# Block attention of the last two mixers: high and low parts in 128-column products, one query block at a time, x kept in DRAM in between

## The chip, the cores and the metric

The kernel runs on one core of one Trainium2 chip. The metric is device time in microseconds (us) of one launch. All data are float32 at the interface. A product that needs float32 accuracy is mostly made here from high and low parts: each operand is split into hi (rounded to the engine's fp32r format) and lo (the rest), and hi x hi, hi x lo and lo x hi are summed in PSUM.

## The reference, cut to what matters

The model has two blocks of two layers each. The change touches the two layers of the second block, whose mixer is a hybrid of three parts. The third part, `nsa_mixer`, is attention with 8 query heads in 2 key groups (4 heads per group, 64 wide), 512 positions, in 4 query blocks of 128. Each query block has three branches: compressed keys (31 of them), selected blocks and a window. With 512 positions, 8 selected blocks of 64 and a window of 512, both latter branches come down to causal attention over all earlier keys.

```python
def hybrid_mixer(h, w_in, ...):
    p = h @ w_in
    za, qb, kb, vb, gb, qc, kcm, vcm, ksl, vsl, kwn, vwn, gc = jnp.split(p, splits, axis=-1)
    y_a = spatial_gating_mixer(za, ...)
    y_b = retention_mixer(qb, kb, vb, gb, ...)
    y_c = nsa_mixer(qc, kcm, vcm, ksl, vsl, kwn, vwn, gc, ...)
    return jnp.concatenate([y_a, y_b, y_c], axis=-1) @ w_out

# in nsa_mixer, for each query block of 128:
p_cmp = masked_softmax(q . k_cmp, ...)   ; o_cmp = p_cmp . v_cmp
p_sel = masked_softmax(q . k_sel, m_sel) ; o_sel = p_sel . v_sel
p_win = masked_softmax(q . k_win, m_win) ; o_win = p_win . v_win
o = g0 * o_cmp + g1 * o_sel + g2 * o_win
```

## The kernel before, in words

The kernel is written for a scheduler that fixes the order of each engine's instructions when it is built; at run time each engine works through its own list in order and waits on semaphores. Activations are kept transposed: 128 features on the partitions by 512 positions, in tiles of 128x512 out of one pool of 71 (names `a`). PSUM has 8 banks of 128x512 (names `p`). Weights come through a ring of raw tiles (`wr`) that ScalarE (ACT) casts to `wh` and VectorE (DVE) completes with `wl`; SyncE (SP) issues nearly all loads, in order.

`hybrid()` does one mixer. It loads five tables (L1413, 256 KB each) and the compression weights `c_w1` (L1423, four of 256 KB), which GpSimd (POOL) multiplies by position columns (L1679) and DVE reduces (L1683). Then come the projections by w_in, and `nsa()`, in which attention runs in steps. A step is a query block `i` and a branch `b` (selected or window): `scores` of one key group, the other work of the mixer (gating, retention: the generator `rest`), the `values` of the step before, scores of the other group, and the softmax (`exponentials`, `weights`). A string `cnt` of digits says how many pieces of `rest` are put at each place, called by `fill()`.

`values(i, b, ...)` walks over the key tiles of 128 keys. For each tile and each key group g it transposes four heads of probabilities (L1790) into one bank, copies the bank to SBUF (L1792, g 0 on ACT, g 1 on DVE) and multiplies by 64 columns of values in plain float32, with the result of both groups in one bank `out[i]`. There are 20 such key tiles in a layer (1+2+3+4 for each of two branches). `blocks(i)` does the compressed branch's scores with 32 keys in high and low parts, `finish(i, ...)` adds its values to `out[i]` and writes `y` as hi (ACT) and lo (DVE). The steps run in the order (3,0), (0,0), (3,1), (1,0), (0,1), (2,0), (2,1), (1,1), so up to three banks `out[i]` are open at a time. `late()` is work that may run beside the last values: the first column tiles of the product by w_out. `post_ln` then takes x, which has been in 8 tiles of SBUF all along (its first use there is a multiplication of `x[0]` on DVE), adds the mixer's result and normalises it.

Of the kernel before, what the change touches and what calls it, by code (L numbers as in the profile page):

```python
# [15 lines left out]
P = 128  # L16
# [87 lines left out]
class Net:  # L104
    def __init__(self, ctx, tc, t):
        self.tc, self.nc, self.t = tc, tc.nc, t
        self.pool = ctx.enter_context(tc.tile_pool(name="sb", bufs=1))
        self.psum = ctx.enter_context(tc.tile_pool(name="ps", bufs=8, space=bass.MemoryType.PSUM))
        self.n = 0
        self.cols = {}  # L110
        self.bg = []
# [1296 lines left out]
    def hybrid(self, l, rhs, first, nxt, start):  # L1408
# [18 lines left out]
        kc = [kcs[:, i * 32:i * 32 + 32] for i in range(4)]  # L1427
# [12 lines left out]
        pb = self.position_parts(l, w1)  # L1440
        q = []
# [34 lines left out]
        both, vals, gt = [self.A(), self.A()], [], self.pool.tile([P, 96], F32, name=self.name("g"), tag="gates", bufs=1)  # L1476

        def others_of_nsa():
            keys(2560)
            yield  # L1480
            for j, ps in enumerate(self.gemm_tok(w, [(2432, 128), (2688, 152)], rhs)):
                o = both[j // 2][:, j % 2 * 256:j % 2 * 256 + 256]
                nc.scalar.copy(o, ps[:, :256])
                vals.append((o[:, :P], o[:, P:]))
                self.act(gt[:, j * 24:j * 24 + 24], ps[:, 256:280], AF.Tanh, scale=0.5)
            self.ts(gt, gt, 0.5, MUL, 0.5, ADD)
            yield
# [15 lines left out]
        def late():  # L1503
            for _ in rest:
                pass
            yield from self.begin(t["w_out2"][l], [(0, 2 * P)], mix, begun, rows=rows)
# [197 lines left out]
    def compressed_heads(self, hid, w2, kc):  # L1704
# [11 lines left out]
        self.doubled(ps[:, :32], *kc)  # L1716
# [21 lines left out]
    def nsa(self, q, kk, vals, gt, kc, vz, tab, ready, rest, late):  # L1738
# [45 lines left out]
        def values(i, b, probs, out):  # L1784
            for kt in range(i + 1):
                pts = []
                for g in range(2):
                    ps = self.PS()
                    for r in range(4):
                        nc.tensor.transpose(ps[:, q4[r]], probs[g][r][:, q4[kt]], self.const("ident"))  # L1790
                    pts.append(self.A())
                    (nc.vector.tensor_copy if g else nc.scalar.copy)(pts[g], ps)  # L1792
                for g in range(2):
                    self.mm(out[group[g], :], vals[kt][b][:, group[g]], pts[g], b == 0 and kt == 0, False, True)
                yield

        def blocks(i):
# [4 lines left out]
            pr, nm, sm = self.A()[:, :256], self.S(8), self.S(8)  # L1802
            for g in range(2):
                ps = self.PS()
                for r in range(4):
                    self.products(ps[:, r * 32:r * 32 + 32], q[r][g], kc, g, q4[i], slice(0, 32), True, True)
                self.tt(r3(pr[:, g * P:g * P + P]), r3(ps[:, :P]), mk(cadd, 4), ADD)
# [10 lines left out]
        def finish(i, pr, out):  # L1818
# [5 lines left out]
            for r in range(4):  # L1824
                for g in range(2):
                    self.mm(out[group[g], q4[r]], vz[:, g * 256 + r * 64:g * 256 + r * 64 + 64],
                            pt[:, g * P:g * P + P], False, r == 3, True)
            if not y:
# [3 lines left out]
                y.extend((self.A(F32R), self.A(F32R)) for _ in range(2))  # L1832
            for r in range(4):
                hi, lo = y[r][0][:, q4[i]], y[r][1][:, q4[i]]
                nc.scalar.copy(hi, out[:, q4[r]])
                self.tt(lo, out[:, q4[r]], hi.bitcast(F32), SUB)


        steps = [(3, 0), (0, 0), (3, 1), (1, 0), (0, 1), (2, 0), (2, 1), (1, 1)]
        before, out, cmp_ = None, {}, {}  # L1840
        cnt = iter("0200112003110110200111000110020301001101")
# [5 lines left out]
        for step in steps + [None]:  # L1847
# [4 lines left out]
            if before:  # L1852
                i, b, probs = before
                if b == 0:
                    out[i] = self.PS()
# [122 lines left out]
```

## Time and profile before

| | |
|---|---|
| median of 3 runs | 3577.85 us (3575.04 to 3580.2) |
| profiled execution | 3580.52 us |
| its span, first to last instruction | 3578.8 us |
| TensorE (PE) busy | 98% |
| VectorE (DVE) busy | 59% |
| ScalarE (ACT) busy | 38% |
| mean granted TensorE clock | 0.992 |

The two hybrid mixers' attention lies at 2261.5 to 2460 us and 2952.5 to 3150 us of the span, some 198 us each. PE is busy through the whole kernel, so a time is saved where PE has less to do, or waits less.

### The profile page before, as it was taken

Reading aid. Unit: us, or ns where it says so; the run is one execution under the profiler, and the core shown is the slowest. Engines: PE = TensorE matmul, PEld = TensorE weight load, DVE = VectorE, ACT = ScalarE, POOL = GpSimd, SP = SyncE. Lnnn points to the kernel's source line nnn. Section 1 sums busy time; section 2 is a strip of 40 time slices with the busy share of each in tenths; the row PEclk is TensorE's granted clock in tenths of the full one; section 3 lists DMA queues with packets and bytes.
Section 4 is the critical chain, followed back from the end, with each engine's and each line's share of the span. In section 5 each row is a group of like instructions: output and inputs, shape, how many; then the busy total and the mean of one; then the engine's idle time right before and its main releaser. Section 6 shows DMA issues by size and latency. Waiting matters only on the chain. (4 is left out here: it accounts for less than half of the span.)

```text
span 3578.8 us, 50232 instructions
## 1 busy us (share of the span) xinstructions
PE 3505.2 (98%) x20564; PEld 2880.8 (80%) x20564; DVE 2127.5 (59%) x3451; ACT 1347.1 (38%) x2198; POOL 143.2 (4%) x189
## 2 busy tenths in 40 slices
PE   8999999999999999999999999999999999999999
PEld 7888877788888888888788888767888887678887
DVE  4442677655434866377676636656655456566565
ACT  3232443223322322257632223543543255445431
POOL 0000000000000000000000001000100020010000
PEclk9999999999999999999999999999999999999999
DMA  4332310013323565321156634211332341013322
GB/s 137 95 96 81 111 43 24 15 60 106 99 95 95 183 188 185 91 77 52 55 149 185 190 112 123 66 31 42 92 97 93 96 113 54 24 54 106 96 98 78
DMA packets 348855, 338.88 MB, mean 95 GB/s; under 512 B 20182, under 2 KB 326929, under 8 KB 348625
## 3 DMA queue, kind: packets, MB, share of 16 engines
q1 hardware_dynamic: 347280, 332.46, 30.7%
q0 software_dynamic: 1344, 3.21, 0.3%
q8 instruction: 161, 2.64, 0.3%
q14 instruction: 70, 0.57, 0.0%
HBM read 333.53 MB, written 2.10 MB: 94 GB/s over the span
## 5 line engine op out<-in xcount | busy, mean ns | idle before, releaser
L152 PE MATMUL p<-a,wh 128*128 128x512 f32 (+1 forms) x8524 | 2430.5, 370 | 18.1 <-ACT a L137 6.2
L152 PEld LDWEIGHTS p<-a,wh 128*128 128x128 f32 x8524 | 1544.9, 190 | 303.2 <-issue 22.6
L152 PE MATMUL p<-a,wl 128*128 128x512 f32 (+1 forms) x4262 | 1564.5, 368 | 0.0
L140 DVE TENSOR_TENSOR wl<-wr,wh 128x1024 fp32r<-128x1024 f32 (+2 forms) x556 | 639.0, 1152 | 730.4 <-ACT wh L252 706.0
L152 PEld LDWEIGHTS p<-a,wl 128*128 128x128 f32 x4262 | 810.2, 190 | 132.4 <-issue 2.7
L252 ACT CAST wh<-wr 128x1024 fp32r<-128x1024 f32 (+2 forms) x518 | 517.3, 1000 | 951.0 <-PE p L152 899.9
L140 DVE TENSOR_TENSOR a<-a,a 128x512 f32<-128x512 f32 (+8 forms) x745 | 439.6, 604 | 89.3 <-ACT a L156 59.8
L152 PE MATMUL p<-a,a 64*64 64x64 f32 (+9 forms) x4360 | 408.0, 275 | 12.6 <-ACT a L1792 3.4
L152 PEld LDWEIGHTS p<-a,a 64*64 64x64 f32 (+3 forms) x4360 | 269.2, 148 | 106.3 <-issue 49.0
L137 ACT ACTIVATE a<-a 128x512 f32<-128x512 f32 (+1 forms) x347 | 194.0, 590 | 344.4 <-DVE a L140 240.1
L140 DVE TENSOR_TENSOR a<-p,a 128x512 f32<-128x512 f32 (+5 forms) x334 | 203.8, 623 | 79.7 <-PE p L152 64.8
L152 PE MATMUL p<-wh,a 128*128 128x256 f32 (+2 forms) x992 | 231.1, 324 | 0.1
L156 ACT CAST a<-a 128x512 fp32r<-128x512 f32 x148 | 91.3, 619 | 269.2 <-DVE a L140 267.2
L152 PEld LDWEIGHTS p<-wh,a 128*128 128x128 f32 x992 | 167.6, 190 | 18.2 <-issue 4.0
L152 PE MATMUL p<-wl,a 128*128 128x256 f32 (+2 forms) x496 | 160.1, 323 | 0.0
L143 DVE SCALAR_TENSOR_TENSOR acc<-wr,s,acc 128x1024 f32<-128x1024 f32 x84 | 107.8, 1283 | 86.3 <-DMA wr<-in_w_ada 86.3
L143 DVE SCALAR_TENSOR_TENSOR a<-p,cols,a 128x510 f32<-128x510 f32 (+1 forms) x176 | 125.1, 744 | 50.8 <-ACT a L137 49.5
L140 DVE TENSOR_TENSOR a<-a,p 128x256 f32<-128x256 f32 (+1 forms) x256 | 116.1, 480 | 34.8 <-PE p L152 34.1
L137 ACT ACTIVATE a<-p 128x512 f32<-128x512 f32 (+2 forms) x152 | 79.6, 551 | 77.3 <-PE p L152 71.5
L152 PEld LDWEIGHTS p<-wl,a 128*128 128x128 f32 x496 | 94.2, 190 | 8.2 <-issue 0.7
L137 ACT ACTIVATE a<-a,cols 128x256 fp32r<-128x256 f32 (+3 forms) x140 | 73.8, 550 | 53.7 <-DVE a L140 53.7
L137 ACT ACTIVATE a<-p,cols 128x512 f32<-128x512 f32 x92 | 68.5, 771 | 59.2 <-PE p L152 59.1
(200 smaller groups left out, 1698.5 us busy)
## 6 DMA issues: line engine op xcount, KB each, us to landing
wr<-in_l_ffn_w_in SPq DMA_DIRECT2D x176, 512.0 KB
wr<-in_w_ada SPq DMA_DIRECT2D x96, 512.0 KB
wr<-in_w_up SPq DMA_DIRECT2D x88, 512.0 KB
wr<-in_l_ffn_w_out SPq DMA_DIRECT2D x68, 512.0 KB
wr<-in_w_in SPq DMA_DIRECT2D x40, 512.0 KB
wr<-in_w_down SPq DMA_DIRECT2D x39, 512.0 KB
wr<-in_l_w_qkv SPq DMA_DIRECT2D x24, 512.0 KB
wr<-in_l_w_in SPq DMA_DIRECT2D x22, 512.0 KB
```

Source lines behind the costliest of these rows:

```text
L137: self.nc.scalar.activation(out, in_, func, bias=bias, scale=scale)
L140: self.nc.vector.tensor_tensor(out, a, b, op=op)
L143: self.nc.vector.scalar_tensor_tensor(out, a, s, b, op0=op0, op1=op1)
L152: self.nc.tensor.matmul(out, lhsT, rhs, start=start, stop=stop, skip_group_check=skip)
L156: self.nc.scalar.copy(hi, src)
L252: self.nc.scalar.copy(hi[:, :m], raw[:, :m])
```

## The change

`values` splits the transposed probabilities into hi (ACT) and lo (DVE) and multiplies both by 128 columns per group: 64 columns of the values' hi beside 64 of their lo. Each group has its own bank, so `out[i]` is two banks, whose two halves are added in `finish` (an ACT copy and a DVE addition) before `y` is split. `blocks` holds the compressed keys as hi beside lo, 64 columns, so that one query tile times 64 columns takes the place of two times 32. The steps run block by block, with a new `cnt`. x is written to DRAM (`away`) at the mixer's start and read back in `late()`.

```diff
+        self.dram = ctx.enter_context(tc.tile_pool(name="dr", bufs=1, space=bass.MemoryType.DRAM))
...
-        kc = [kcs[:, i * 32:i * 32 + 32] for i in range(4)]
+        kc = [kcs[:, i * 64:i * 64 + 64] for i in range(2)]
...
         pb = self.position_parts(l, w1)
+        away = self.dram.tile([D, T], F32, name=self.name("away"))
+        for k in range(KD):
+            nc.sync.dma_start(away[k * P:(k + 1) * P, :], self.x[k])
...
-                o = both[j // 2][:, j % 2 * 256:j % 2 * 256 + 256]
-                nc.scalar.copy(o, ps[:, :256])
-                vals.append((o[:, :P], o[:, P:]))
+                o = self.A(F32R)
+                ov = o.rearrange("p (b g s d) -> p g s b d", b=2, g=2, s=2)
+                pv = ps[:, :256].rearrange("p (b g d) -> p g b d", b=2, g=2)
+                for g in range(2):
+                    nc.scalar.copy(ov[:, g, g], pv[:, g])
+                    self.tt(ov[:, g, 1 - g], pv[:, g], ov.bitcast(F32)[:, g, g], SUB)
+                vals.append((o[:, :256], o[:, 256:]))
...
+            self.x = [self.A() for _ in range(KD)]
+            for k in range(KD):
+                nc.sync.dma_start(self.x[k], away[k * P:(k + 1) * P, :])
             yield from self.begin(t["w_out2"][l], [(0, 2 * P)], mix, begun, rows=rows)
...
-                    pts.append(self.A())
-                    (nc.vector.tensor_copy if g else nc.scalar.copy)(pts[g], ps)
+                    pts.append(self.split(ps))
                 for g in range(2):
-                    self.mm(out[group[g], :], vals[kt][b][:, group[g]], pts[g], b == 0 and kt == 0, False, True)
+                    for u, part in enumerate(pts[g]):
+                        self.mm(out[g], vals[kt][b][:, g * P:g * P + P], part, b == 0 and kt == 0 and u == 0, False, True)
...
+            ps = self.PS()
             for g in range(2):
-                ps = self.PS()
                 for r in range(4):
-                    self.products(ps[:, r * 32:r * 32 + 32], q[r][g], kc, g, q4[i], slice(0, 32), True, True)
-                self.tt(r3(pr[:, g * P:g * P + P]), r3(ps[:, :P]), mk(cadd, 4), ADD)
+                    o = (g * 4 + r) * 64
+                    self.mm(ps[:, o:o + 64], q[r][g][:, q4[i]], kc[g], o == 0, False, True)
+            parts = ps.rearrange("p (r u n) -> p u r n", u=2, n=32)
+            self.tt(r3(pr), parts[:, 0], mk(cadd, 8), ADD)
+            self.tt(r3(pr), parts[:, 1], r3(pr), ADD)
...
+            o = self.A()
+            for g in range(2):
+                nc.scalar.copy(o[group[g]], out[g][group[1 - g]])
+                self.tt(o[group[g]], out[g][group[g]], o[group[g]], ADD)
             for r in range(4):
                 hi, lo = y[r][0][:, q4[i]], y[r][1][:, q4[i]]
-                nc.scalar.copy(hi, out[:, q4[r]])
-                self.tt(lo, out[:, q4[r]], hi.bitcast(F32), SUB)
-        steps = [(3, 0), (0, 0), (3, 1), (1, 0), (0, 1), (2, 0), (2, 1), (1, 1)]
+                nc.scalar.copy(hi, o[:, q4[r]])
+                self.tt(lo, o[:, q4[r]], hi.bitcast(F32), SUB)
+        steps = [(i, b) for i in (1, 2, 3, 0) for b in range(2)]
-        cnt = iter("0200112003110110200111000110020301001101")
+        cnt = iter("00011111111111110111101111011001101111000")
```

In the changed kernel the helper `split` stands at L155, its cast at L157 and its subtraction at L141; the transposes at L1803, the store of x at L1445, its reload at L1518, and the tables' and `c_w1`'s loads at L1414 and L1424.

Of the PE list of the first hybrid mixer, one place in `values` where two key tiles follow each other. Before (`p_19325`, `p_19332`, `p_19341`, `p_19348` take transposes, `p_19324` is `out[i]`):

```order
L1790 MATMUL p_19332<-consts,a_19139 128x128
L152 MATMUL p_19324<-a_19330,a_19013 64x512
L152 MATMUL p_19324<-a_19337,a_19013 64x512
L1790 MATMUL p_19341<-consts,a_19035 128x128
L1790 MATMUL p_19341<-consts,a_19038 128x128
L1790 MATMUL p_19341<-consts,a_19041 128x128
L1790 MATMUL p_19341<-consts,a_19044 128x128
L1790 MATMUL p_19348<-consts,a_19130 128x128
```

And after, at such a place (`p_20089`, `p_20098`, `p_20111`, `p_20120` take transposes; `p_19828` and `p_19829` are the two banks of `out[i]`):

```order
L153 MATMUL p_19828<-a_20094,a_19237 128x512
L153 MATMUL p_19829<-a_20103,a_19237 128x512
L153 MATMUL p_19828<-a_20095,a_19237 128x512
L1803 MATMUL p_20111<-consts,a_19877 128x128
L1803 MATMUL p_20111<-consts,a_19880 128x128
L1803 MATMUL p_20111<-consts,a_19883 128x128
L1803 MATMUL p_20111<-consts,a_19886 128x128
L153 MATMUL p_19829<-a_20104,a_19237 128x512
L1803 MATMUL p_20120<-consts,a_19980 128x128
```

Two plain float32 products became four in high and low parts, of which the last (lo of group 1, `a_20104`) stands behind the next key tile's first four transposes.

Of the SP list, the head of the first hybrid mixer. Before, the tables and `c_w1` follow three loads of w_in:

```order
L236 DMA wr_18724<-in_w_in 128x8x128
L1413 DMA a_18583<-in_hybrid_tab 128x512
L1413 DMA a_18584<-in_hybrid_tab 128x512
L1413 DMA a_18585<-in_hybrid_tab 128x512
L1413 DMA a_18586<-in_hybrid_tab 128x512
L1413 DMA a_18587<-in_hybrid_tab 128x512
L1423 DMA a_18593<-in_c_w_k 128x8x64
L1423 DMA a_18594<-in_c_w_k 128x8x64
```

After, seven of the eight stores of x stand between; the last three of them, and what follows, are:

```order
L1445 DMA away_18629<-a_131 128x512
L1445 DMA away_18629<-a_138 128x512
L1445 DMA away_18629<-a_145 128x512
L1414 DMA a_18585<-in_hybrid_tab 128x512
L1414 DMA a_18586<-in_hybrid_tab 128x512
L1414 DMA a_18587<-in_hybrid_tab 128x512
L1414 DMA a_18588<-in_hybrid_tab 128x512
L1414 DMA a_18589<-in_hybrid_tab 128x512
L1424 DMA a_18595<-in_c_w_k 128x8x64
L1424 DMA a_18596<-in_c_w_k 128x8x64
```

Each store waits until DVE has written its tile of x, so the loads behind wait for that too.

Of the DVE list, the end of the first hybrid mixer. Before, `a_101` and `a_108` are x in SBUF, and the four `y` rows are the last lo parts:

```order
L1823 COPY a_20864<-p_20861 128x256
L147 TENSOR_SCALAR a_20918<-a_101 128x512
L147 TENSOR_SCALAR a_20921<-a_108 128x512
L140 TENSOR_TENSOR wl_21026<-wr_21023,wh_21025 128x1024
L140 TENSOR_TENSOR y_19959<-p_20025,y_19959 128x128
L140 TENSOR_TENSOR y_19960<-p_20025,y_19960 128x128
```

After, `a_20957` and `a_20958` are x read back from DRAM:

```order
L1839 COPY a_20996<-p_20993 128x256
L141 TENSOR_TENSOR wl_21175<-wr_21172,wh_21174 128x1024
L141 TENSOR_TENSOR a_21006<-p_20820,a_21006 64x512
L141 TENSOR_TENSOR a_21006<-p_20821,a_21006 64x512
L148 TENSOR_SCALAR a_21067<-a_20957 128x512
L148 TENSOR_SCALAR a_21070<-a_20958 128x512
L141 TENSOR_TENSOR y_19700<-a_21006,y_19700 128x128
```

Two additions that join the halves of `out` stand there now, and the reloaded x is asked for ahead of the last lo parts.

## Rows read from the trace of the kernel before

**Rows 1.** The page: busy us, share of the span and instructions of each engine.

```profile
PE 3505.2 (98%) x20564; PEld 2880.8 (80%) x20564; DVE 2127.5 (59%) x3451; ACT 1347.1 (38%) x2198; POOL 143.2 (4%) x189
```

**Rows 2.** Windows, both attention stretches: us, busy (x) by engine, PEclk, DMA share, GB/s.

```profile
2261.50:2460.00 198.50, 193.50 (x1144) 133.04 (x1144) 124.13 (x297) 94.31 (x245) 7.85 (x6) 0.99 0.13 35
2952.50:3150.00 197.50, 191.85 (x1144) 132.69 (x1143) 123.63 (x292) 94.29 (x245) 7.85 (x6) 1.00 0.13 35
```

**Rows 3.** PE groups by form, 2261.5 to 2460: xcount | busy, mean ns | idle before.

```profile
L152 PE MATMUL p<-a,a 128*64 128x512 f32 x80 | 35.1, 638 | 1.8 <-ACT a L1792 1.7
L1790 PE MATMUL p<-consts,a 128*128 128x128 f32 x160 | 22.8, 278 | 2.2 <-ACT a L137 1.5 <-ACT a L1792 0.7
...
L152 PE MATMUL p<-a,a 128*128 128x32 f32 x64 | 8.2, 267 | 0.0
```

**Rows 4.** The same view, 2952.5 to 3150.

```profile
L152 PE MATMUL p<-a,a 128*64 128x512 f32 x80 | 33.7, 616 | 2.5 <-ACT a L1792 1.7 <-DVE a L1792 0.6
```

**Rows 5.** Timeline of PE: start, us, line, operation, count, [idle before].

```profile
2300.46 0.62 PE L152 MATMUL p<-a,wh 128*128 128x512 f32 x2
...
2301.16 0.62 PE L152 MATMUL p<-a,wh 128*128 128x512 f32 x2
...
2301.93 2.42 PE L152 MATMUL p<-a,a 128*64 128x512 f32 x8
2304.28 0.73 PE L152 MATMUL p<-a,wh 128*128 128x512 f32 x2
...
2325.33 1.86 PE L152 MATMUL p<-a,a 128*128 128x32 f32 x16
...
2401.21 1.04 PE L1790 MATMUL p<-consts,a 128*128 128x128 f32 x8
2402.49 1.62 PE L152 MATMUL p<-a,a 128*64 128x512 f32 x4 [0.24 <-ACT a L1792]
2404.04 1.09 PE L1790 MATMUL p<-consts,a 128*128 128x128 f32 x8
```

**Rows 6.** ACT and DVE groups by form, 2261.5 to 2460.

```profile
L1792 ACT COPY a<-p 128x512 f32<-128x512 f32 x20 | 11.5, 584 | 35.2 <-PE p L1790 35.2
...
L1792 DVE COPY a<-p 128x512 f32<-128x512 f32 x20 | 13.6, 687 | 8.0 <-PE p L1790 8.0
L1764 DVE TENSOR_REDUCE s<-p 128x1 f32<-128x512 f32 x16 | 10.4, 684 | 3.8 <-PE p L152 3.8
...
L140 DVE TENSOR_TENSOR a<-p,a 128x512 f32<-128x512 f32 x10 | 6.7, 688 | 1.9 <-PE p L152 1.8
```

**Rows 7.** Timelines of SP, POOL, DVE and PE at the head of the first hybrid mixer.

```profile
2183.65 2.73 SPq L1413 DMA_DIRECT2D a<-in_hybrid_tab  x5
...
2198.60 4.25 POOL L1679 TENSOR_TENSOR a<-a,cols 128x512 f32<-128x512 f32 x4
...
2197.17 5.97 DVE L140 TENSOR_TENSOR a<-a,a 128x256 fp32r<-128x256 f32 x3
...
2206.85 1.08 DVE L140 TENSOR_TENSOR a<-a,a 128x256 f32<-128x256 f32 x3
...
2223.31 4.06 DVE L1683 TENSOR_REDUCE a<-a 128x64 f32<-128x512 f32 x4
...
2202.01 0.58 PE L152 MATMUL p<-a,wh 128*128 128x256 f32 x1 [1.34 <-DVE a L140]
...
2205.11 1.14 PE L152 MATMUL p<-a,wh 128*128 128x256 f32 x2 [0.39 <-ACT a L453]
```

**Rows 8.** Windows, the head of the first hybrid mixer (columns as in Rows 2).

```profile
2196.80:2262.00 65.20, 62.49 (x411) 54.93 (x411) 41.52 (x63) 27.27 (x45) 9.07 (x14) 0.92 0.31 83
```

**Rows 9.** Timelines of POOL and DVE at the head of the second hybrid mixer.

```profile
2909.09 4.07 POOL L1679 TENSOR_TENSOR a<-a,cols 128x512 f32<-128x512 f32 x4
...
2912.20 0.68 DVE L1670 COPY st<-p 64x512 f32<-64x512 f32 x1 [5.84 <-PE p L152]
```

**Rows 10.** DMA view of 2180 to 2240: GB/s in 40 slices of 1.5 us.

```profile
GB/s 259 112 249 283 389 366 319 231 218 119 60 161 82 147 0 11 0 0 0 0 0 11 279 248 255 256 0 0 11 0 0 0 0 0 212 143 159 191 239 65
```

More of the change, by code (lines that the diff above doesn't have):

```diff
@@ L1475, in hybrid @@
         vz = self.compressed_heads(hid, w2, kc)
-        both, vals, gt = [self.A(), self.A()], [], self.pool.tile([P, 96], F32, name=self.name("g"), tag="gates", bufs=1)
+        vals, gt = [], self.pool.tile([P, 96], F32, name=self.name("g"), tag="gates", bufs=1)
         def others_of_nsa():
@@ L1715, in compressed_heads @@
                 self.mm(pv[r * 32:r * 32 + 31, g * 64:g * 64 + 64], hid[64:128, cs], w2[64:128, 0:64])
-        self.doubled(ps[:, :32], *kc)
+        self.doubled(ps[:, :32], *[kc[g][:, i * 32:i * 32 + 32] for i in range(2) for g in range(2)])
         vzv = vz.rearrange("p (g r d) -> p g r d", g=2, r=4)
@@ L1825, in finish @@
                 for g in range(2):
-                    self.mm(out[group[g], q4[r]], vz[:, g * 256 + r * 64:g * 256 + r * 64 + 64],
+                    self.mm(out[g][group[g], q4[r]], vz[:, g * 256 + r * 64:g * 256 + r * 64 + 64],
                             pt[:, g * P:g * P + P], False, r == 3, True)
@@ L1854, in nsa @@
                 if b == 0:
-                    out[i] = self.PS()
+                    out[i] = self.PS(), self.PS()
                 work = values(i, b, probs, out[i])
```

## The prediction

> **What bounds the kernel now.** I began with the page: PE is busy for 98% of the span, DVE for 59%, ACT for 38% [rows 1]. So only PE's own work, or a wait on PE, is worth anything, and the other engines count where PE stands behind them. Then I read the windows of the two attention stretches, which hold nearly all that the change touches. There PE is idle for 198.5 - 193.5 = 5.0 us and 197.5 - 191.85 = 5.65 us, at a clock of 0.99 and 1.00 [rows 2]. That idle time is not the whole of the waiting: a matmul's row also covers what it waits for inside a group, and for that I went to the groups by form [rows 3, 4] and to starts in the timeline [rows 5]. Last I read the head of the first mixer, where the clock is only 0.92 [rows 8].
>
> What the groups show: the values' products (64 columns by 512) cost 35.1 us of busy time in the first layer and 33.7 in the second, in 80 rows for 40 products, so one plain float32 product leaves two rows [rows 3, 4]. They have the only waits on the eviction copies.
>
> **Values, PE's work.** Eight such rows back to back take from 2301.93 to 2304.28, 2.35 us, 0.294 each [rows 5]. So 80 cost 23.5 us with nothing to wait for. After, a layer has 80 products of 128 columns by 512 in fp32r. Of that kind three take from 2300.46 to 2301.16, 0.70 us, 0.233 each [rows 5]; 80 cost 18.7. PE's work falls by 4.8 us a layer.
>
> **Values, the waits.** A lone key tile now goes: eight transposes at 2401.21, a wait of 0.24, four product rows at 2402.49, the next at 2404.04 [rows 5]. The products take 1.55 us where 4 x 0.294 = 1.18 is work, so 0.24 + 0.37 = 0.61 us is waiting. Over 20 key tiles that is 12.2 us a layer, and values with their waits cost 23.5 + 12.2 = 35.7.
>
> After, each bank of transposes gives two tiles, hi by ACT and then lo by DVE, which reads hi. I price hi at ACT's copy of the same shape, 0.584, and lo at DVE's subtraction out of PSUM, 0.688 [rows 6]. The copy now ends some 1.25 us after the first transpose starts (2402.49 - 2401.21 = 1.28 with the start of the product). From there, at full clock: the first product (hi, group 0) starts at 1.28; hi of group 1 is ready at 1.83, so the second starts at 1.87; lo of group 0 is ready at 1.94, so the third follows at once at 2.10; lo of group 1 is ready at 2.63. The order puts the next tile's transposes or scores ahead of that fourth product, 0.44 us or more, so it starts at 2.77 and waits for nothing. The waits are 0.40 behind the transposes and 0.36 ahead of the second product, 0.76 us for a tile with nothing between. Where scores or other products lie between transposes and products, as at many tiles in the new order, both shrink. For the second of two tiles in a row the same walk gives 0.61. I take 0.6 a tile, between 0.4 and 0.76: 12 us a layer. Values after cost 18.7 + 12 = 30.7, so 5 us less a layer, 10 in all. The bounds from 0.4 and 0.76 are 9 and 1.8 us less a layer.
>
> **Blocks.** Sixteen of the 32-column products take 1.86 us, 0.116 each [rows 5]; there are 64 a layer [rows 3], 7.4 us. Of 64 columns there will be 32. The trace has no such row, but the transposes with 128 columns take 1.04 / 8 = 0.13 at most [rows 5], so a price between 0.116 and 0.13 holds: 3.7 to 4.2 us. I take the nearer, 0.116: 3.7 us less a layer. The added DVE additions are few (one of 128x256 a block in place of two halves' worth) and stand in front of a softmax that is used a step later, so I cost them at nothing; if that cover is gone, each is under 0.69 us, 2.8 us a layer.
>
> **The added ACT and DVE work.** A layer gets 20 more evictions on each engine: 40 casts in place of 20 copies on ACT, 40 subtractions in place of 20 copies on DVE. With the splits of the values and the joins of `out`, ACT goes from 94.3 to about 111 us and DVE from 124.1 to about 144 of some 190 [rows 2, 6]. DVE's subtractions stand in its list among the score reductions (0.684 each) [rows 6] and the scalings; behind a late subtraction wait PE's fourth product and the next step's softmax. The waits of PE on DVE and ACT in the softmax (1.5 us of the transposes' 2.2 idle is on the scaling, ACT's L137) [rows 3] can grow. I put 1.5 us a layer on that, from 0 to 5.
>
> **The end of a query block.** `finish` gets two copies on ACT and two additions on DVE ahead of `y`, 2 x 0.584 and 2 x 0.688 at most, with the second copy beside the first addition about 1.9 us. The order puts twelve products by w_out (12 x 0.233 = 2.8 us) between the last values and the first use of the last `y`. So I cost it at nothing; without that cover it is 1.9 us a layer. For the other three query blocks `y` is not needed for a long time.
>
> **x through DRAM.** 2 MB go out and 2 MB come back in a layer. In the attention stretches DMA is 0.13 busy [rows 2], so there is room. The reload stands ahead of one w_out load in SP's list and can start when the last gate column's products are done; from there PE has about 35 products of 512 columns and some 100 short ones up to the last `y`, 35 x 0.233 plus some 9, about 17 us. At the 319 to 389 GB/s that four slices in a row moved at the head [rows 10], 2 MB take 5.4 to 6.6 us. Hidden, at nothing. The stores at the head push the tables and `c_w1` back: they were issued from 2183.65 [rows 7], and now wait for x, on which DVE still works in the row at 2206.85 [rows 7]. With the stores that is 4.3 MB, 11 to 14 us at that rate, much of it ahead of the last store, so the weights of the compression land near 2213 instead of before 2198.60, when POOL starts on them. What needs them is POOL's multiplication and then the reductions on DVE, which start at 2223.31 [rows 7], so PE does not see it.
>
> **The head.** One thing gains there. DVE's three additions of 128x256 at 2197.17 last 5.97 us where three of the same size take 1.08 later [rows 7]. They are stuck exactly while POOL multiplies (2198.60 to 2202.85) [rows 7], and PE waits 1.34 on DVE and 0.39 on ACT behind it [rows 7]. In the second mixer POOL's multiplication falls into a DVE gap of 5.84 us and holds up nothing [rows 9]. With `c_w1` later, POOL's work moves to about 2215, past this tail. The gain is at least those two waits, 1.73 us, and at most the 4.9 us by which DVE's op is too long; I take 3, once. The Trainium skill (SBUF — State Buffer, section "Who interferes with whom") says that a DVE instruction with two SBUF inputs and a GpSimd instruction that reads SBUF lock each other out for a whole instruction. The trace agrees with the one lock that it shows. By that rule the multiplication, once moved, would hold up whatever two-input work of DVE is then under way, the `wl` subtractions for w_in, by up to its own 4.25 us, and if PE had no slack there the head's gain would be spent and the time by the median would be 3564.
>
> **The sum.** Values -10, blocks -7.4, engines' load +3, head -3: -17.4 us. Nearly all of it, (4.8 + 3.7) x 2 = 17, is work that PE no longer has; the waits on both sides come out alike. On the profiled execution's 3580.5 that gives 3563. That execution lies 2.7 us above the median of the three runs, so by the runs' median 3577.85 it is 3560. The forecast's own range, from the bounds above, is 3550 to 3570.
>
> **Rivals.** *The evictions become the wait.* For it: every key tile now passes through two engines in series, 0.584 + 0.688 twice, in lists that also carry the softmax. Against it: lo of group 1 is ready ahead of its use in the walk above, and DVE still has a quarter of its time free. PE saves (4.8 + 3.7) x 2 + 3 = 20 us apart from waits; over 40 key tiles that is 0.5 us a tile. If the wait grows from 0.61 to about 1.1 us a tile, which one score reduction (0.684) ahead of most lo parts would do, nothing is left: 3571 to 3585. The Trainium skill (Perfetto Trace Analysis, section "Matmuls") asks to rotate PSUM banks so that evictions overlap with the next group's products. Here a transposed bank is held until its lo is done, and `out` takes two, which speaks for this rival; no row of the kernel before shows a wait for a bank.
>
> *Slower.* The same DVE list decides: from 1.3 us a tile on, two reductions ahead of each lo, the kernel is slower; at 1.5 us it is (1.5 - 1.1) x 40 = 16 us, 3594. For it: in a softmax step DVE gets four reductions at once. Against: now the g 1 copy on DVE stands in the same list and costs only 0.37 a tile.
>
> *The parking of x holds up the loads.* The w_in loads stand behind all stores and table loads. If they land more than 9 us later than now in each layer, PE waits for them, and the gain is gone; at 15 us it is 3590. The rate in [rows 10] speaks against it.
>
> *A larger gain.* If other work covers the tiles' waits wholly, values cost 18.7 of 35.7 us: -34, -7.4, -3 is 3533; halfway it is 3545. For it: the new string puts a piece of other work at nearly every place, and the first steps have only two key tiles, so that the first wait (1.5 us, on scalings) shrinks.
>
> **Chances.** Forecast 0.52; larger gain 0.22; evictions eat it 0.14; slower by DVE's list 0.07; slower by the parked x 0.05. What a measurement of this kernel can tell from no change is about 0.2%, 7 us. Faster is the first two, 0.74; the same 0.14; slower 0.12. The range leaves about a tenth on each side: half of the larger gain below 3543, and most of the slower cases above 3582.
>
> **What will show it.** In the windows of the attention stretches the span should fall by 5 to 10 us a layer; the values' group should read 128x512, 80 a layer, with 0.6 us a tile of waiting in their starts; 32 products of 64 columns near 0.116; DVE near 145 us. At the head DVE's three additions near 1.1 us, and POOL's row near 2215. If the scores or transposes wait on DVE where they did not, the first rival holds; if PE waits on `wh` or `wl` soon after the head, the third; if DVE stands before the first scaling of x in `post_ln` for a DMA, the reload is late. I am wrong above all if the walk through one tile misses what stands ahead of lo in DVE's list.

## The result, and the profile after

The changed kernel takes 3620.97 us (median of 4 runs, 3614.46 to 3628.54) against 3578.57 of the kernel before (4 runs): a ratio of 1.0121 with a 95% interval of 1.0109 to 1.0133. It is 42 us slower where 18 us less were forecast. Its profiled execution has a span of 3626.8 us.

The windows of the head of the first mixer and of its attention (us, busy us and instructions of PE, PEld, DVE, ACT and POOL, granted clock, DMA share, GB/s), kernel after:

```profile
2183.00:2262.00 79.00, 76.52 (x536) 69.36 (x535) 48.74 (x97) 34.15 (x63) 12.62 (x21) 0.98 0.51 145
2262.00:2470.00 208.00, 182.64 (x1036) 138.99 (x1035) 134.97 (x308) 103.67 (x262) 7.76 (x6) 0.88 0.14 42
2276.00:2312.00 36.00, 25.55 (x123) 18.66 (x122) 28.20 (x81) 15.79 (x47) 4.87 (x5) 0.67 0.11 30
2312.00:2450.00 138.00, 127.52 (x713) 93.88 (x712) 84.63 (x180) 68.96 (x163) 0.00 (x0) 0.95 0.12 34
2450.00:2475.00 25.00, 20.57 (x113) 16.38 (x112) 17.51 (x50) 11.73 (x37) 2.89 (x1) 0.73 0.19 70
```

Beside [rows 2], PE is now idle for 208 - 182.64 = 25.4 us in the attention, where it was 5.0 in a stretch of much the same length, and the granted clock there is 0.88 in place of 0.99. More than half of the idle time and most of the lost clock lie at the two ends: in the first 36 us PE is idle for 10.5 us at a clock of 0.67, in the last 25 for 4.4 at 0.73. The 138 us between lose another 10.5 at 0.95. DVE and ACT are far from full, as forecast.

The stage is longer by about what the whole kernel lost. The first transpose of the first mixer's attention starts at 2281.12 (before, 2285.30), the first load of w_up behind that mixer is issued at 2490.65 (before, 2468.27): 209.5 us in place of 183.0. In the second mixer it is 207.5 in place of 182.2, so the two stages lose some 52 us, where the spans of the profiled executions differ by 48.0; the first stage starts 4.2 us earlier. The groups of PE by form in the first attention, kernel after, 2262 to 2505 (columns as in [rows 3]), show where it waits:

```profile
L153 PE MATMUL p<-a,a 128*128 128x512 f32 x120 | 49.1, 485 | 11.1 <-ACT a L157 9.0 <-DVE a L141 1.4 <-ACT a L138 0.6
...
L1803 PE MATMUL p<-consts,a 128*128 128x128 f32 x160 | 27.4, 312 | 4.3 <-ACT a L138 3.6 <-DVE a L141 0.6
...
L153 PE MATMUL p<-a,a 128*128 128x384 f32 x32 | 9.6, 414 | 3.1 <-ACT a L1783 2.9
```

The first row holds the 80 new products (and 40 others of the same shape): 9.0 us of waiting on the casts to hi (L157), where the old products waited 1.7 on ACT's copies [rows 3]. The second is mostly the transposes' wait for the softmax's scaling on ACT, which grew from 1.5 [rows 3] to 3.6. The third are scores that wait until ACT's exponentials (L1783) have emptied a bank; no score waited for that before.

How such a wait comes about is seen in the timelines of PE, ACT and DVE at the first step's values, kernel after (the third row is PE at the last step's):

```profile
2281.12 1.94 PE L1803 MATMUL p<-consts,a 128*128 128x128 f32 x8 [2.69 <-ACT a L138]
...
2285.53 1.65 PE L153 MATMUL p<-a,a 128*128 128x512 f32 x4 [1.85 <-ACT a L157]
...
2468.20 0.80 PE L153 MATMUL p<-a,a 128*128 128x512 f32 x1 [3.14 <-ACT a L157]
...
2282.24 0.59 ACT L157 CAST a<-p 128x512 fp32r<-128x512 f32 x1
2284.59 0.42 ACT L138 ACTIVATE a<-a 128x256 f32<-128x256 f32 x1 [1.75 <-DVE a L141]
2284.91 0.57 ACT L157 CAST a<-p 128x512 fp32r<-128x512 f32 x1
...
2283.33 0.43 DVE L141 TENSOR_TENSOR a<-a,s 128x256 f32<-128x256 f32 x1 [0.84 <-POOL s L1548]
```

The second cast to hi does not follow the first. Between them stands an activation of the gating (the "other work" that the string of fills put there), which waits 1.75 us on DVE, which in turn waits on POOL. The cast's data are ready (the eight transposes of the row at 2281.12 end at 2283.06); its place in ACT's list is not. PE waits 1.85 us for it. At the last step it is the same: the cast stands behind two casts of other work, for which ACT waits 3.07 us on DVE, and PE waits 3.14.

### The profile page after: what moved, and what is told of

Read it like the earlier page. It is cut to its first block, busy times and chain, and to the rows that moved or that the text cites. A ratio compares the mean times of both kernels' runs of the same rounds, so it can differ in the third digit from the quotient of the medians.

```text
span 3626.8 us, 50315 instructions
## 1 busy us (share of the span) xinstructions
PE 3510.5 (97%) x20500; PEld 2912.0 (80%) x20500; DVE 2159.8 (60%) x3523; ACT 1379.1 (38%) x2262; POOL 142.7 (4%) x189
## 5 line engine op out<-in xcount | busy, mean ns | idle before, releaser
L153 PE MATMUL p<-a,wh 128*128 128x512 f32 (+1 forms) x8524 | 2433.2, 370 | 19.9 <-ACT a L138 6.2
L141 DVE TENSOR_TENSOR wl<-wr,wh 128x1024 fp32r<-128x1024 f32 (+2 forms) x556 | 638.9, 1152 | 740.3 <-ACT wh L253 714.7
L141 DVE TENSOR_TENSOR a<-a,a 128x512 f32<-128x512 f32 (+8 forms) x761 | 437.9, 591 | 84.7 <-ACT a L157 57.2
L153 PE MATMUL p<-a,a 64*64 64x64 f32 (+10 forms) x4296 | 411.4, 274 | 43.0 <-ACT a L157 17.8
L153 PEld LDWEIGHTS p<-a,a 64*64 64x64 f32 (+3 forms) x4296 | 288.1, 153 | 129.2 <-issue 39.5
L141 DVE TENSOR_TENSOR a<-p,a 128x512 f32<-128x512 f32 (+6 forms) x430 | 269.6, 642 | 103.2 <-PE p L153 59.1
L157 ACT CAST a<-a 128x512 fp32r<-128x512 f32 x148 | 91.3, 619 | 266.4 <-DVE a L141 266.3
L141 DVE TENSOR_TENSOR a<-a,p 128x256 f32<-128x256 f32 (+1 forms) x256 | 116.3, 481 | 29.6 <-PE p L153 28.8
```

What stands on the lines that cost most here:

```text
L141: self.nc.vector.tensor_tensor(out, a, b, op=op)
L153: self.nc.tensor.matmul(out, lhsT, rhs, start=start, stop=stop, skip_group_check=skip)
L157: self.nc.scalar.copy(hi, src)
```

## The experiments

Each was timed in alternation with the kernel before on the same chip. The table gives the difference of the medians, and PE's idle time and clock in the window of 2262 to 2470 us where a reading rests on them. The edits and expectations follow.

| run | order of steps | string | values | median us | against before | idle, clock |
|---|---|---|---|---|---|---|
| before | old | old | plain | 3577 | 0 | 5.0, 0.99 |
| after | new | new | by parts | 3621.0 | +42.4 | 25.4, 0.88 |
| e1 | old | old | plain, x parked | 3570.4 | -6.9 | 7.0, 1.00 |
| e2 | new | new | plain, x parked | 3619.0 | +41.8 | 14.8, 0.92 |
| e3 | new | new | plain, two banks | 3628.4 | +51.2 | 18.0, 0.90 |
| e4 | new | new | hi alone | 3585.3 | +8.0 | 23.1, 0.90 |
| e5 | old | new | plain | 3605.1 | +28.6 | 11.4, 0.94 |
| e6 | new | old | plain | 3587.3 | +10.8 | 7.4, 0.97 |
| e7 | old | old | plain, new blocks | 3564.3 | -12.2 | 6.6, 0.99 |
| e8 | 3, 0, 2, 1 | new | by parts | 3594.0 | +17.5 | 20.0, 0.93 |
| e9 | new | old | by parts | 3609.6 | +32.5 | 17.6, 0.88 |
| e10 | 3, 0, 2, 1 | old | by parts | 3586.0 | +8.9 | 19.9, 0.94 |
| e11 | 2, 3, 1, 0 | old | by parts | 3607.2 | +30.1 | |
| e12 | new | new | by parts, tile behind | 3609.3 | +32.2 | 23.3, 0.89 |
| e13 | new | new | by parts, filler | 3626.5 | +49.4 | 22.0, 0.94 |
| e14 | 3, 0, 2, 1 | old | plain, new blocks | 3574.0 | -3.1 | 12.4, 0.98 |
| e15 | 3, 0, 2, 1 | old | by parts, tile behind | 3569.8 | -7.3 | 19.8, 0.96 |
| e16 | 3, 0, 2, 1 | moved | by parts, tile behind | 3574.2 | -2.6 | |
| e17 | old | old | plain, new blocks, tile behind | 3544.3 | **-32.5** | 6.8, 1.00 |
| e18 | old | old | as e17, groups apart | 3559.0 | -18.8 | 6.6, 1.00 |

All from e1 on have x parked. The theory at the start: the order and the string leave PE without cover. The rivals: the evictions in two parts, the banks, and the parked x. The new order without the parked x was not tried, and neither were the products by parts in the old order of steps.

**e1, x parked alone.** The kernel before, with these lines of the change and nothing else:

```diff
+        for k in range(KD):
+            nc.sync.dma_start(away[k * P:(k + 1) * P, :], self.x[k])
...
+            self.x = [self.A() for _ in range(KD)]
+            for k in range(KD):
+                nc.sync.dma_start(self.x[k], away[k * P:(k + 1) * P, :])
```

> The kernel before, with x stored to DRAM and read back, and nothing else changed. If the parked x costs the time (loads held back, reload late), this run takes over 15 us more than before's 3578 us. If the loss lies in the attention steps (their order, the evictions, the banks), it takes 3571 to 3579 us: no loss, and perhaps the 3 to 4 us that POOL's multiplication no longer costs DVE at the head of the first mixer.

Ratio 0.998 (0.997 to 0.9989): faster by 6.9 us, and the side effect at the head is where: the first transpose of the first mixer's attention starts 7.6 us earlier than before (2277.66 for 2285.30). The rows of DVE and POOL there, kernel after, answer to [rows 7]:

```profile
2198.34 1.08 DVE L141 TENSOR_TENSOR a<-a,a 128x256 fp32r<-128x256 f32 x3
...
2215.30 4.19 POOL L1692 TENSOR_TENSOR a<-a,cols 128x512 f32<-128x512 f32 x4 [15.52 <-DMA a<-in_c_w_k]
```

POOL's multiplication now waits for `c_w1` and runs at 2215.30; DVE's three additions take 1.08 us in place of 5.97. In e1 the clock of the head is 0.98 (2183 to 2262; before, 0.94), and that of the attention's first 36 us, 2276 to 2312, is 1.00 (before, 0.95).

The parked x is not free everywhere, though. At the head of the second mixer, kernel after, the stores and tables stand ahead of a load of w_in, which SP issues at 2936.47; ACT waits 6.13 us for it to land before it can cast, and PE waits behind that:

```profile
2945.54 0.50 PE L153 MATMUL p<-a,wl 128*128 128x512 f32 x1 [2.36 <-DVE wl L141]
```

The same wait is 1.45 us in e1. PE has none there in the kernel before.

**e2, the order and the string, with plain values.** e1 plus two lines:

```diff
-        steps = [(3, 0), (0, 0), (3, 1), (1, 0), (0, 1), (2, 0), (2, 1), (1, 1)]
+        steps = [(i, b) for i in (1, 2, 3, 0) for b in range(2)]
-        cnt = iter("0200112003110110200111000110020301001101")
+        cnt = iter("00011111111111110111101111011001101111000")
```

> The run before it plus the new order of steps and the new string of fills; values and blocks stay as in the kernel before (plain float32, one bank). If the order block by block is the cause (short steps follow each other, and PE has nothing to cover the softmax), this run already takes 3600 us or more. If the evictions in two parts or the two banks are the cause, it stays within 10 us of the run with x parked alone.

48.7 us above e1 (both against before): these two lines alone bring the kernel to the changed kernel's time. The evictions in two parts are not needed for that loss. What PE waits for is still an eviction, the plain copies of L1800. The values' group, window 2262 to 2510, and one of its waits with what stands ahead of the copy on ACT:

```profile
L153 PE MATMUL p<-a,a 128*64 128x512 f32 x80 | 39.2, 706 | 7.7 <-ACT a L1800 5.1 <-DVE a L1800 2.5
...
2457.01 1.97 PE L153 MATMUL p<-a,a 128*64 128x512 f32 x2 [3.54 <-ACT a L1800]
...
2453.86 1.22 ACT L157 CAST a<-a 128x512 fp32r<-128x512 f32 x2 [3.81 <-DVE a L141]
```

In e1 the same group is busy for 33.6 us and waits 2.5. The copy for 2457.01 starts at 2456.37, behind these two casts of other work and four exponentials. At the first step PE waits 2.55 us for DVE's copy, which starts at 2276.03 behind the gating's chain, itself held 0.84 us by POOL. So it is the mechanism of the changed kernel's first step: a piece of other work ahead of the eviction in an in-order list.

**e3, two banks.** e2 with `out[i] = self.PS(), self.PS()`, one bank for each key group.

> The run before it, with the result of each key group in a bank of its own (64 of 128 partitions used), so that two banks are held through a query block; the products and their evictions are those of before. If the lack of banks is the cause, it takes 10 us or more above the run with the new order alone. If not, under 5 us.

9.4 us more than e2, at the edge of what was asked for. The edit does more than its expectation says: with two banks, `finish` also writes `y` one group at a time, so ACT's casts and DVE's subtractions for it double; those named `y`, which are half of them, go from 4.4 us busy to 8.7 in the first mixer's attention. The second bank costs 9.4 us at most; it is not the main cause.

**e4, hi alone.** The changed kernel, the low parts of the probabilities left out:

```diff
-                    pts.append(self.split(ps))
+                    pts.append([self.A(F32R)])
+                    nc.scalar.copy(pts[g][0], ps)
```

> The changed kernel without the low parts of the transposed probabilities: 80 subtractions on DVE and 80 of the 160 products are left out, 80 x 0.233 = 18.6 us of PE's work over both layers. If the chain hi, lo, product is the cause of the loss, the time falls far more than by that work, below 3580 us from 3621. If the order of the steps is the cause, it falls by the work and little more, to 3595 to 3605 us.

34 us less (against before) for an estimated 18.6 us of work left out. It falls between the two expectations: some 16 us of the low parts' cost is not work, but the idle time (23.1) and clock (0.90) hardly change, so most of the waits do not hang on the low parts.

**e5 and e6, order and string apart.** e1 with the new string and the old steps, and with the new steps and the old string.

> The kernel before with x parked (3570 us), with the new string of fills and the old order of steps. If the string (other work spread evenly, little of it in the first steps) makes the loss, this takes 3600 us or more. If the order of the steps does, it stays within 10 us of 3570.

> The other half: x parked, the new order of steps, the old string. If the order makes the loss, 3605 to 3625 us as with both. If the string does, within 10 us of 3570. If only the two together fit each other, both halves lose more than both at once (3619).

Against e1: the string +35.5, the steps +17.7, both +48.7. With plain values the string alone costs twice what the steps alone cost. e5 has what its first reading asks; e6 lies between its readings. The sum of the digits is 29 in both strings; what differs is where they stand. The old string gives the first two steps 3 and 6 pieces, two of them right behind the first step's first softmax; the new one gives them 2 and 5, none until both groups' first softmax is issued, and none in the last two places of the last step.

**e7, the blocks by parts.** e1 with the change's `blocks` and `kc`.

> x parked, and the blocks with high and low keys side by side (32 products of 64 columns in place of 64 of 32 a layer), in the old order of steps. If a product costs the same 0.116 us with 64 columns, 7 us under the run with x parked alone: 3563 us. If the blocks lie beside other waits, no change.

5.3 us less than e1 (both against before), near the 7 of the first reading. In the kernel after, one query block's products read:

```profile
2363.97 0.97 PE L153 MATMUL p<-a,a 128*128 128x64 f32 x8
2365.54 0.70 PE L153 MATMUL p<-a,a 128*128 128x512 f32 x1 [0.59 <-ACT a L138]
```

Eight go by in 0.98 us (2365.54 - 0.59 - 2363.97), 0.12 each.

**e8 to e11, other orders with the changed products.** e8 has the blocks in the order `(3, 0, 2, 1)`; e9 the changed kernel with the old string; e10 both; e11 `(2, 3, 1, 0)` with the old string.

> The changed kernel with another order of query blocks, 3, 0, 2, 1, each still finished before the next. If the loss comes from which steps stand first and last (two short ones at the start, two of one key tile at the end, with nothing to cover their softmax), it falls by 20 us or more, to 3600 or less. If it comes from one block being open at a time whichever it is, it stays within 10 us of 3621.

> The changed kernel (3621 us) with the string of fills of the kernel before. Against the run with x parked, the new steps and the old string (3587), it differs only in the products by parts, their banks and the blocks. If the string makes most of the loss here too, 3580 to 3592. If the string was written for these evictions and covers them, the time stays at 3615 or more.

> Blocks in the order 3, 0, 2, 1 (3594 us with the new string) with the old string. If order and string each cost time by themselves, 3565 to 3580 us; if the long first block already cured what the string costs, 3590 or more.

> Blocks in the order 2, 3, 1, 0 with the old string. It starts long and ends with the one-tile steps. If only the start matters, as fast as 3, 0, 2, 1 within 5 us; if the end matters (the last values have nothing behind them), 5 to 10 us slower than that.

e8 is 25 us faster than the changed kernel, as its first reading asks: which block comes first and last matters. e9 is only 10 us faster, where 29 to 41 were expected if the string made most of the loss: what the old string saves the plain values it does not save the new ones. So on equal order and string (e9 against e6) the products by parts, with their banks and blocks, cost 21.7 us. e10 lies between its two readings: against the changed kernel the order alone gives 24.9 us, the string alone 9.9, both 33.5, so each costs time by itself, but what is left is more than the first reading has. e11 shows that a long start is not enough; with the one-tile block at the end it is 21 us above e10, where 5 to 10 were expected.

**e12, products one tile behind.** The changed kernel; each tile's products are issued behind the next tile's transposes:

```diff
+            last = None
             for kt in range(i + 1):
...
-                for g in range(2):
-                    for u, part in enumerate(pts[g]):
-                        self.mm(out[g], ...)
+                if last:
+                    product(*last)
+                last = kt, pts
                 yield
+            product(*last)
```

> The changed kernel (3621 us) with each key tile's products moved behind the next key tile's transposes, so that hi and lo have a tile's time to be made. If the chain transposes, hi, lo, product inside a tile is what PE waits for, the time falls by 15 us or more. If the waits stand at the steps' starts (softmax) and in the order, under 8 us.

10 us less: between the two expectations. The chain inside a tile is part of the loss, and the ends of the attention keep theirs (clock still 0.89).

**e13, filler products.** The changed kernel with this ahead of the transposes:

```diff
+                    for _ in range(2 if g else 0 if kt else 6):
+                        self.mm(ps[:, :384], self.masks[:, :P], self.masks, True, True, True)
```

> The changed kernel with needless products put in PE's list (bf16, 384 columns, overwritten by the transposes behind them): six ahead of the first key tile of each step, two between a tile's two groups of transposes, 88 a layer, 0.16 us each by their columns, 28 us over both layers. If the slow clock after the waits is most of the loss, they fill waits, the clock in the attention stretch rises from 0.88 to 0.95 or more, and the time falls in spite of them. If the waits themselves are the loss, they lie in them or add to them: 3621 to 3650.

The needless work, 28 us by the estimate, costs 7 us (against before), and the clock in the attention is 0.94 in place of 0.88. (Its rows are busy for 19.8 us in the first mixer, so 28 for both may be low.) So some 21 us or more of it were paid out of waits and a faster clock, but the clock alone does not give the time back: the second expectation holds by the time, the first nearly by the clock.

**e14 and e15.** e7 with the blocks in the order 3, 0, 2, 1; and e10 with the products one tile behind.

> x parked, blocks by parts, plain values in one bank, order of blocks 3, 0, 2, 1 and the old string: against the changed products in the same order and string (3586 us). If the products by parts save time once the order is the same, this is slower, 3590 or more; if they lose more to their waits than the 10 us of PE's work that they save, it is faster, 3565 to 3580.

> Products a tile behind, order of blocks 3, 0, 2, 1, old string (3586 us without the tile's delay). If the chain inside a tile is what is left there, 3560 to 3572 us, about the plain version's best or better; if banks run short by it (four transposed banks beside two of the result), no gain or a loss.

Plain values in e10's order are 12 us faster than by parts: the parts lose more to their waits than they save. With the delay, the products by parts gain 16 us and come out below before, at a ratio of 0.9981 (0.9972 to 0.9991).

**e16, the string moved.** e15 with `01011 11112` for the first ten digits.

> The last run (order 3, 0, 2, 1, products one tile behind; 3570 us) with the other work of the first two steps spread as single pieces (string 01011 11112 in place of 02001 12003). If the 4.6 us wait in each layer stands there because two pieces follow each other without other work between, 5 to 12 us less: 3558 to 3565. If the piece only waits elsewhere, no change within 4 us.

3574.2 us, 4.7 more than e15 against before: not faster. The wait moved elsewhere: PE's 4.61 us at 2293.22 in e15 are gone, and e16 has 3.25 at 2283.43 and 1.42 at 2302.14. How much of e15's remaining waiting another string could cover stays open.

**e17, plain products one tile behind.** e7 with the delay of e12.

> x parked, blocks by parts, the old order and string, plain products (3564 us) with the tile's delay. If it is the two-part eviction that needs the delay, no change within 4 us, since PE waits only some 0.6 us a tile there. If each tile's chain costs the plain version too, 8 to 12 us less: 3552 to 3556.

The fastest version: 3544.31 us, a ratio of 0.9909 (0.9893 to 0.9926), and 20 us less than e7 where at most 12 were thought possible. PE's idle time does not explain it, 6.8 us against 6.6. The values' own group does. PE groups by form, window 2262 to 2470, in e7:

```profile
L153 PE MATMUL p<-a,a 128*64 128x512 f32 x80 | 33.6, 628 | 1.9 <-ACT a L1800 1.7
```

And in e17:

```profile
L153 PE MATMUL p<-a,a 128*64 128x512 f32 x80 | 26.8, 613 | 0.5 <-DVE a L1805 0.3 <-ACT a L1805 0.2
```

The same 80 rows are busy for 26.8 us in place of 33.6, while one row is about as long as it was (613 and 628 ns). They lie over each other more. With 7.1 us in the second mixer (26.0 in place of 33.1) that is 13.9 of the 20 us. The kernel before had shown it already, in a place that the forecast did not use. Timeline of PE, kernel before, a tile whose two products were both ready:

```profile
2455.57 1.08 PE L152 MATMUL p<-a,a 128*64 128x512 f32 x4
2456.58 0.50 PE L152 MATMUL p<-a,wh 128*128 128x512 f32 x1
```

Four rows in 1.01 us, where the lone tile of [rows 5] took 1.55. There DVE's copy for group 1 ended at 2402.98, 0.49 us after group 0's product had begun, so the second product lay beside half of the first only. Group 0 has its values in columns 0 to 63 and group 1 in columns 64 to 127.

**e18, the two groups apart.** e17 with the two products of a tile no longer neighbours:

```diff
                     (nc.vector.tensor_copy if g else nc.scalar.copy)(pts[g], ps)
-                if last:
-                    product(*last)
+                    if last:
+                        product(*last, (g,))
```

> The fastest run so far (plain products one tile behind, 3544 us), with the products of the two key groups no longer next to each other: group 0's stands behind the next tile's first four transposes, group 1's behind the next four. In the order as built 42 of the 96 products of this shape then stand alone between others, against 12. If two neighbours share TensorE's columns and take little more time than one, 30 more lone products at about 0.45 us each cost 8 to 15 us: 3552 to 3560. If each product takes its own time wherever it stands, no change within 4 us.

3558.99 us, 13.7 more than e17 against before, inside what the shared columns ask for. The values' group in e18:

```profile
L153 PE MATMUL p<-a,a 128*64 128x512 f32 x80 | 33.4, 614 | 0.3 <-ACT a L1805 0.2
```

Busy time is back at 33.4 us with only 0.3 us of idle time ahead of it: no wait has come back, only the neighbourhood has gone. One product that stands alone between transposes, timeline of PE, e18:

```profile
2282.73 1.07 PE L153 MATMUL p<-a,a 128*64 128x512 f32 x2
2283.73 0.66 PE L1803 MATMUL p<-consts,a 128*128 128x128 f32 x4
```

Its two rows take 1.00 us to the next instruction, as long as the four of two ready neighbours (1.01). Two products of 64 columns in different halves, issued one after the other, run side by side. The Trainium skill (TensorE: Matmul & The Clock Gate, section "Part 3: Packing small matmuls — row/col tiling") describes this for outputs that lie in distinct column groups; the trace agrees, 1.01 us for two products against 1.00 for one.

The kernel before has 12 such lone products of 40 in its first attention, e18 has 18. The delay is worth something without the neighbours too: e18 is still 6.5 us faster than e7 (both against before), and what those come from was not tested.

## Why the prediction was wrong, step by step

**Values, PE's work: wrong.** The forecast took eight old rows in 2.35 us, 0.294 each, as "with nothing to wait for" and reckoned 4.8 us less work a layer. Those rows were not free of waiting (DVE's copy for the second product ended 0.43 us after the first had begun), and two rows of different groups overlap when both are ready. At 1.01 us a ready tile it is 20.2 a layer, against 4 x 0.233 = 0.93 a tile, 18.7 a layer, for the new products: 1.5 us less work a layer, not 4.8. In e17 two ready tiles in a row went by in 1.87 us once (2336.71 to 2338.58), and by that nothing is left. The 128-column products fill the array, but the old ones shared it already. Of a lone tile's 1.55 us, 0.54 is lost overlap. e17 takes 6.8 and 7.1 us of such losses back in the two layers without changing a product.

**Values, the waits: wrong.** The walk through one tile gave ACT and DVE nothing else to do, and 0.6 us a tile. In the lists a cast to hi stands behind the gating's activation and its chain over DVE and POOL, as the rows of 2282 to 2285 show; the casts to hi cost 9.0 us of waiting in the first attention. On equal order and string the new values cost 21.7 us more than the plain ones (e9 against e6, the blocks' gain included), 12 us in the better order (e10 against e14); forecast were 10 us less for the values and 7.4 for the blocks. The last sentence of the prediction had named what stands ahead of lo as the risk; it was above all what stands ahead of hi, on ACT (9.0 us against 1.4 on DVE).

**The order and the string: no term at all.** The prediction gave 1.5 us a layer for the added ACT and DVE work, and where it spoke of the string and the steps, in its rival of a larger gain, it took them for a gain ("the first steps have only two key tiles, so that the first wait (1.5 us, on scalings) shrinks"). e2 shows that the two lines cost 48.7 us with plain values. In e2 the attention loses 7.8 us of PE to idle time against e1, 5.2 of it in the values' waits on their copies, and 8% of 208 us, at most 16.6, to a slower clock: an estimate of up to 24.4 for a layer, beside half of 48.7 measured. How much overlap of neighbours is lost as well can't be told from the clock. Where the string puts other work ahead of an eviction on ACT or DVE, PE waits for that work. Short steps at the start have few products of their own to cover it, and in the changed kernel the transposes' waits on the scaling, 1.5 us over the whole attention before [rows 3], are 2.69 us at the first step alone. At the end the one-tile block leaves the last values with a wait of 3.14 us (3.54 in e2).

**The slow clock: not priced.** Here the waits cost more than their length: the first 36 us ran at 0.67. e13 shows that filling waits brings the clock from 0.88 to 0.94.

**Two banks.** Named as what speaks for the first rival, without a price. e3: 9.4 us at most. That no row before shows a wait for a bank was misread: in [rows 3] the transposes, which read no copy, wait 0.7 us on ACT's copies (L1792), which empty their banks.

**Blocks: right.** 7.4 us forecast over both layers, 5.3 measured.

**The head: right in its mechanism, too small.** 3 us forecast, 6.9 measured (e1): DVE's additions fell from 5.97 to 1.08, and the clock stayed up in the head and behind it. That the move of POOL's multiplication makes the whole gain is read from the rows; no run moves it alone. The multiplication at 2215.30 met no `wl` subtraction that PE waited for; the 3564 that the prediction gave for that case did not come.

**x through DRAM: right on the whole, not at nothing.** e1 as a whole gains. But a load of w_in held up behind the stores costs PE a wait of 2.36 us at the second head (1.45 in e1), the sign that the prediction gave for its third rival, at a small price. (The rate of 319 to 389 GB/s stood in three slices in a row, not four [rows 10]; nothing hangs on it.)

**The rivals.** The one that ended slower put 3594 us on DVE's list at 1.5 us a tile. It had the sign, but not the place: the longest waits lie at the first and last steps, behind other work on ACT, and with plain values order and string alone make such waits (e2).

So the step that failed is above all the missing price of order and string, and with it the free lists of ACT and DVE in the walk through one tile. The changed kernel's +42.4 adds up as order and string +48.7 with x parked at -6.9, and the products by parts, with blocks, another +0.6 in that order. That the gains of the blocks and of the lighter products are lost again to banks and casts is argued from e3 and the rows, not shown by a run. These parts do not simply add (the same products cost 21.7 us more under the old string), so how the 42 us divide between them is not settled.

## What to carry to other kernels

An order of steps and a list of where other work goes are costs of their own: a change that rewrites them should be split, and the order run with the old arithmetic first. A price read from "back to back" rows is a floor only if both operands were ready; look for the shortest instance of the group, and for instructions that overlap in it. A chain of two evictions in a busy in-order list wants a tile of distance between producer and consumer: the same delay gave 10, 16 and 20 us in three versions (some 14 of the 20 by bringing neighbours together), and made the old products, with x parked and the new blocks, the fastest of all.

## What the runs showed of the hardware

Two float32 products of 64 columns in opposite halves of the array, next to each other in PE's list and both ready, take 1.01 us together; one alone takes 1.00 (e18). Where the second's operand came 0.49 us after the first had begun, the two took 1.55. Taking neighbours apart costs 13.7 us over the kernel.

Three DVE additions with both operands in SBUF took 5.97 us while POOL multiplied for 4.25 us [rows 7]; with the multiplication moved away, 1.08.

With waits of 1.85 and 2.69 us in it, the attention's start ran at a granted clock of 0.67 over 36 us (between the two levels of 1.2 and 2.4 GHz): by estimate, 36 x 0.33, up to 12 us of PE's time, beside 10.5 us of idling.
